# Two of a Strassen set's four differences in one VectorE step, on a decoder layer that keeps TensorE busy

## The chip, the cores and the metric

The kernel runs on one core of a Trainium2 chip. The metric is the device time of one execution in microseconds; the time before is the median of 3 runs. Engines are named as in the profile: PE is TensorE, PEld its weight loads, DVE is VectorE, ACT is ScalarE, POOL is GpSimd, and SP is SyncE, whose queue (SPq) issues most of the transfers. What can be told from no change on this kernel is about 0.2% (3.4 us).

## The reference

One decoder layer on 256 tokens of width 2048, all in float32, cut to what matters here:

```python
x = layer_norm(ALPHA * x + 0.5 * swiglu_ffn(x, ffn1...), ln1)      # FFN 1, inner width 5632
u = x @ w_in + b_in                                                # 2048 -> 3328
attn_out = sliding_window_attention_with_sinks(q, k, v, sinks)     # 16 heads of 64, window 128
conv_out = silu(layer_norm(depthwise_conv31(a * sigmoid(gate))))   # 1024 channels
x = layer_norm(ALPHA * x + concat(attn_out, conv_out) @ w_out + b_out, ln2)
x = layer_norm(ALPHA * x + 0.5 * swiglu_ffn(x, ffn2...), ln3)      # FFN 2
```

Here `swiglu_ffn(x) = (silu(x @ w_gate) * (x @ w_up)) @ w_down`. The weights (some 330 MB) are read once from memory, and every matrix product must be accurate to more than one pass of TensorE gives, so each operand is kept as a high part and a low part.

## The kernel before

**High and low parts.** Every weight unit of 128 x 1024 is loaded raw, cast by ACT to a high part (`hi`, line 171), and DVE makes its low part (`lo` = raw - hi, line 175). A product is then three matmuls (`mm3`, lines 678 to 680: hi x hi, lo of the weights, low of the activations), each 128 x 512. `hi` and `lo` are rings of 8 tiles.

**Strassen sets.** In both FFNs many units are not used as they are. Two raw units A = (a0 | a1) and B = (b0 | b1), halves of 512 columns, make a set (kind "S", 80 sets in all) whose seven products stand for eight; plain pairs of units are of kind "C". A set yields four units u0 to u3, made by the four jobs `zeroth`, `first`, `second` and `third` of the class `Steps`:

- u0 = (a0 | a1): a cast and a low part.
- u1 = (b0 - a0 | b1 - b0 + a0): the two differences t0 and t1 go into two tiles `sum` of 512 columns (tag "bc"), t1 from t0, then two casts and two low parts of 512.
- u2 = (b1 - b0 | b1): the difference is written over b0 in B's place (`more`), then one cast and one low part of 1024.
- u3 = (a1 - t1): written over a1, then a cast and a low part of 512.

In the trace, line 189 is a difference, 171 a cast and 175 a low part; `raw` is a unit of kind C, `more` one of a set's raw places, and `sum` a tile of t0 or t1. `more` has four places, room for two sets.

**What sets the order.** Nothing is scheduled by a compiler: each engine runs its instructions in the order in which the Python code issues them. While TensorE's products are issued, `pace` keeps a model of DVE's backlog (`vector` adds to it, `tensor` takes off) and issues the next job whenever the backlog is under 1.2 us. A low part is not issued with its cast but kept in `pending`, and goes out with a later job (`flush`) or when TensorE takes the unit (`take`). Between these DVE also has to empty the sums of the products (line 1078 in the up projection, line 939 in the down projection), to multiply the gates (`ht`, 1026), to transpose them in blocks (`hr`, 1040), and to split the result into `hh` and `hl` (1053 and 1054) when it is back from a round trip through memory (`far`, `hf`, issued by POOL).

**The mixer between the FFNs.** There the weights `in_win` are loaded by SP into four `raw` buffers, cast by ACT (line 254), and POOL makes the low parts (line 257). POOL also works the residual off, chunk by chunk (`residuals`, line 594: with a scale row `rg`, a shift row `rb` and a bias row `ro`, 512 columns each). These rows are loaded by SP too (`row_chunk`, line 476), into tiles of the same tag "bc" as the sums: six buffers of 512 columns before. ACT empties every projection (`part`, line 1259), does the exponentials of attention (line 1377) and scales its probabilities `pr` (line 1391) before TensorE transposes them (`tp`, line 1397).

Of the kernel before, what the change touches and what calls it, by code (L numbers as in the profile page):

```python
# [18 lines left out]
P = 128  # L19
# [35 lines left out]
BC = 6  # L55
# [29 lines left out]
class Steps:  # L85
# [66 lines left out]
    def load_set(self, n):  # L152

        k = 2 * (self.begun % 2)
        raws = [self.places[:, k], self.places[:, k + 1]]
# [3 lines left out]
        for raw, src in zip(raws, self.sources[n][0]):  # L159
            self.nc.sync.dma_start(raw, src)  # L160
# [3 lines left out]
    def upper(self, n, raw):  # L164

        pair = [self.pool.tile([P, 1024], F32R, tag=t, name=f"{t}{n}", bufs=RING) for t in ("hi", "lo")]
        raw = raw if isinstance(raw, list) else [raw]
        w = raw[0].shape[1]
        parts = [[x_, *(t[:, i * w : (i + 1) * w] for t in pair)] for i, x_ in enumerate(raw)]
        for x_, hi, lo in parts:  # L170
            self.nc.scalar.copy(hi, x_)  # L171

        def lower():
            for x_, hi, lo in parts:
                self.nc.vector.tensor_tensor(out=lo, in0=x_, in1=hi.bitcast(F32), op=ALU.subtract)  # L175
            self.vector(1.14 if len(raw) * w == 1024 else 0.6)
            self.ready[n] = pair
            while self.whole in self.ready:
                self.whole += 1
# [8 lines left out]
    def sub(self, out, a, b):  # L188
        self.nc.vector.tensor_tensor(out=out, in0=a, in1=b, op=ALU.subtract)  # L189
        self.vector(0.6)  # L190

    def zeroth(self, n, raws):
        zero = self.upper(n, raws[0])
        self.flush()
        raws.append(zero)

    def first(self, n, raws):
        a, b = ([r[:, :512], r[:, 512:]] for r in raws[:2])
        t = [self.act.tile([P, 512], F32, tag="bc", name=f"sum{n}", bufs=BC) for _ in range(2)]
        raws.append(t)  # L200
        self.sub(t[0], b[0], a[0])
        self.sub(t[1], b[1], t[0])
        self.pending = [raws[2], self.upper(n, t)]

    def second(self, n, raws):
        b = [raws[1][:, :512], raws[1][:, 512:]]
        self.sub(b[0], b[1], b[0])
# [3 lines left out]
    def third(self, n, raws):  # L211
        a1 = raws[0][:, 512:]
        self.sub(a1, a1, raws[3][1])
# [134 lines left out]
def hybrid_layer(  # L348
# [100 lines left out]
    def keep_tokens():  # L449
        for n in range(2 * NC_):  # L450
            b, cols = n // NC_, slice(n % NC_ * 512, (n % NC_ + 1) * 512)

            def one(b=b, cols=cols):
                t = act.tile([P, 512], F32, tag="bc", name="some", bufs=BC)
# [18 lines left out]

    def row_chunk(r, c, name, queue=nc.sync):
        t = act.tile([P, 512], F32, tag="bc", name=name, bufs=BC)
# [390 lines left out]
    def by_sums(kinds, blocks, out, shared):  # L866
# [17 lines left out]
        for n, kind in enumerate(kinds):  # L884
            if kind == "S":
# [4 lines left out]
                product(6, at("S2"), u[1], 1)  # L890
                u.append(st.take())
                product(7, at("S3"), u[2], 0)
# [304 lines left out]
def mixer(tc, nc, env):  # L1197
# [7 lines left out]
    with tc.tile_pool(name="mix", bufs=1) as pool:  # L1205
# [5 lines left out]
        bk = act.tile([P, 512], F32, tag="bc", name="bk", bufs=BC)  # L1211
# [386 lines left out]
```

## Time and profile before

| what | value |
|---|---|
| median of 3 runs | 1677.49 us (1676.08 to 1678.96) |
| the profiled execution | 1677.86 us, of which the span of instructions is 1676.10 us |
| PE busy | 1655.2 us, 99% of the span |
| DVE busy | 1485.0 us, 89% |
| ACT busy | 959.2 us, 57% |
| POOL busy | 322.6 us, 19%, nearly all of it in the mixer |
| granted TensorE clock | 0.998 |
| transfers | 377.31 MB, 225 GB/s |

A row of a group gives line, engine, operation, output and inputs, shapes and count, then the busy time and the mean of one in ns, then the idle time of the engine just before them and what ended it. A row of the timeline gives start, length, engine, line and operation, with the idle time before it in brackets; `x2` is two instructions merged into one row, the length from the first start to the last end. Ends of instructions on DVE overlap the next start a little, so what an instruction costs in a row of others is the step from start to start. A row of a window gives busy time and count of instructions for each engine.

### The profile page before, as it was taken

The page shows a single profiled execution, that of the slowest core. Times are in us where ns is not written, and L with a number is a line of the kernel's source. Part 1 is how long each engine was busy: PE and PEld are TensorE (multiplying, and loading weights), DVE is VectorE, ACT ScalarE, POOL GpSimd, SP SyncE. Part 2 cuts the span into 40 slices and gives each one's busy share as a digit, 9 for nine tenths or more (in the row PEclk, how much of TensorE's full clock was granted, in tenths as well). Part 3 has the DMA queues.
Part 4 walks back from the last instruction along what each step waited for, and adds up shares of the span by engine and source line. Part 5 has one row for each costly group of instructions (what it writes and reads, how often), then busy time and mean ns, then how long its engine had stood idle before and what let it go on. Part 6 is the DMA issues. An engine that isn't in the chain of part 4 may idle for free. (4 is left out here: it accounts for less than half of the span.)

```text
span 1676.1 us, 22034 instructions
## 1 busy us (share of the span) xinstructions
PE 1655.2 (99%) x7617; PEld 1369.7 (82%) x7617; DVE 1485.0 (89%) x2221; ACT 959.2 (57%) x1346; POOL 322.6 (19%) x302
## 2 busy tenths in 40 slices
PE   9999999999999999999999999999999999999996
PEld 7888888877778888888888888888888888788885
DVE  7899899999899998958888768899999999999987
ACT  6555555656555555676665466555555555555552
POOL 0100000111110001178996201000000000000012
PEclk9999999999999999999999999999999999999999
DMA  8666677677788567656655568666776666776675
GB/s 312 241 223 230 208 248 250 192 245 248 237 244 254 208 217 250 220 186 190 200 179 158 192 224 286 245 221 225 251 235 221 215 215 216 250 238 219 210 243 157
DMA packets 110976, 377.31 MB, mean 225 GB/s; under 512 B 13968, under 2 KB 14096, under 8 KB 110736
## 3 DMA queue, kind: packets, MB, share of 16 engines
q1 hardware_dynamic: 94032, 329.50, 56.9%
q0 software_dynamic: 16112, 45.10, 10.7%
q10 hardware_dynamic: 720, 1.31, 0.3%
q8 instruction: 59, 0.97, 0.2%
q14 instruction: 53, 0.43, 0.1%
HBM read 349.64 MB, written 27.26 MB: 225 GB/s over the span
## 5 line engine op out<-in xcount | busy, mean ns | idle before, releaser
L175 DVE TENSOR_TENSOR lo<-raw,hi 128x1024 fp32r<-128x1024 f32 x300 | 352.2, 1220 | 32.7 <-ACT hi L171 32.5
L678 PE MATMUL sum<-hi,xcat 128*128 128x512 f32 x956 | 372.0, 389 | 0.0
L679 PE MATMUL sum<-lo,xcat 128*128 128x512 f32 x956 | 371.9, 389 | 0.0
L680 PE MATMUL sum<-hi,xcat 128*128 128x512 f32 x956 | 371.9, 389 | 0.0
L171 ACT CAST hi<-more 128x1024 fp32r<-128x1024 f32 (+1 forms) x240 | 217.9, 908 | 251.6 <-DVE more L189 221.8
L171 ACT CAST hi<-raw 128x1024 fp32r<-128x1024 f32 x300 | 298.7, 1047 | 35.8 <-DMA raw<-in_wd 18.2
L175 DVE TENSOR_TENSOR lo<-more,hi 128x1024 fp32r<-128x1024 f32 (+1 forms) x240 | 244.3, 1041 | 20.3 <-ACT hi L171 20.2
L678 PE MATMUL sum<-hi,hh 128*128 128x512 f32 x580 | 226.5, 391 | 2.1 <-DVE part L939 2.1
L680 PE MATMUL sum<-hi,hl 128*128 128x512 f32 x580 | 226.0, 390 | 1.5 <-DVE hl L1054 1.5
L679 PE MATMUL sum<-lo,hh 128*128 128x512 f32 x580 | 226.0, 390 | 0.6 <-DVE lo L175 0.6
L254 ACT CAST hi<-raw 128x1024 fp32r<-128x1024 f32 (+1 forms) x156 | 158.6, 1029 | 93.1 <-PE acc L680 40.9
L678 PEld LDWEIGHTS sum<-hi,xcat 128*128 128x128 f32 x956 | 179.4, 188 | 37.6 <-issue 0.3
L680 PEld LDWEIGHTS sum<-hi,xcat 128*128 128x128 f32 x956 | 179.4, 188 | 37.5
L679 PEld LDWEIGHTS sum<-lo,xcat 128*128 128x128 f32 x956 | 179.4, 188 | 37.1
L257 POOL TENSOR_TENSOR lo<-raw,hi 128x1024 fp32r<-128x1024 f32 x73 | 176.0, 2438 | 110.8 <-ACT hi L254 103.8
L1045 POOL DMA_DIRECT2D far<-hr x88 | 49.1, 563 | 761.4 <-DVE hr L1040 761.3
L171 ACT CAST hi<-sum 128x512 fp32r<-128x512 f32 x160 | 98.9, 622 | 165.4 <-DVE sum L189 144.4
L678 PEld LDWEIGHTS sum<-hi,hh 128*128 128x128 f32 x580 | 108.8, 188 | 27.2 <-ACT hi L171 2.9
L680 PEld LDWEIGHTS sum<-hi,hl 128*128 128x128 f32 x580 | 108.9, 188 | 25.0 <-DVE hl L1054 2.4
L679 PEld LDWEIGHTS sum<-lo,hh 128*128 128x128 f32 x580 | 108.9, 188 | 24.1 <-DVE lo L175 1.7
L257 DVE TENSOR_TENSOR lo<-raw,hi 128x1024 fp32r<-128x1024 f32 (+1 forms) x83 | 98.1, 1201 | 23.9 <-ACT hi L254 23.6
L1078 DVE TENSOR_TENSOR part<-sum,part 128x512 f32<-128x512 f32 x152 | 101.4, 687 | 12.6 <-PE sum L680 7.8
(210 smaller groups left out, 2548.4 us busy)
## 6 DMA issues: line engine op xcount, KB each, us to landing
raw<-in_wu SPq DMA_DIRECT2D x244, 512.0 KB, 5.1
raw<-in_wd SPq DMA_DIRECT2D x120, 512.0 KB, 5.3
more<-in_wu SPq DMA_DIRECT2D x104, 512.0 KB, 6.8
more<-in_wd SPq DMA_DIRECT2D x56, 512.0 KB, 7.5
raw<-in_win SPq DMA_DIRECT2D x52, 512.0 KB, 4.2
raw<-in_wout SPq DMA_DIRECT2D x32, 512.0 KB, 3.8
far<-hr POOLq DMA_DIRECT2D x88, 128.0 KB, 2.7
hf<-far POOLq DMA_DIRECT2D x22, 512.0 KB, 4.9
```

The costliest lines, as they stand in the source:

```text
L171: self.nc.scalar.copy(hi, x_)
L175: self.nc.vector.tensor_tensor(out=lo, in0=x_, in1=hi.bitcast(F32), op=ALU.subtract)
L254: nc.scalar.copy(hi, raw)
L257: eng.tensor_tensor(out=lo, in0=raw, in1=hi.bitcast(F32), op=ALU.subtract)
L678: nc.tensor.matmul(ps, s_hi, m_hi, start=start, stop=False)
L679: nc.tensor.matmul(ps, s_hi, m_lo, start=False, stop=False)
L680: nc.tensor.matmul(ps, s_lo, m_hi, start=False, stop=stop)
L1045: nc.gpsimd.dma_start(far[:, :, t].rearrange("f r n -> r f n"), hr[32 * t : 32 * t + 32])
L1078: nc.vector.tensor_tensor(out=out, in0=ps, in1=other, op=ALU.add)
```

## The change

The set's units are cut in another way. One DVE instruction of 128 x 1024 makes d = (b0 - a0 | b1 - b0), reading B and a view of the two left halves (a0, b0) together. Then b0 is overwritten by (b1 - b0) + a0, so that u1 = d = (b0 - a0 | b1 - b0) and u2 = (b1 - b0 + a0 | b1). u1 so has one cast and one low part of 1024 in place of two of 512 each. The two products that use b1 - b0 and b1 - b0 + a0 change places (`product(7...)` and `product(6...)`). `zeroth` no longer flushes; `first` issues d, then flushes what is pending (the low part of the unit before), and then the step that depends on d. The tiles of tag "bc" become three of 1024 columns in place of six of 512: `row_chunk` hands out their halves in turn (`spare`), two row chunks to a tile; `some` and `bk` take a whole tile for one half.

```diff
--- before.py
+++ after.py
@@ -52,7 +52,7 @@
 PACE = 0.68
 STOCK = 3
 LAST = 8
-BC = 6
+BC = 3
 ORDER = "ccqqccqqccqqcc"
 CAP = 1.6
 FILL = 4.0
@@ -152,11 +152,11 @@
     def load_set(self, n):
 
         k = 2 * (self.begun % 2)
-        raws = [self.places[:, k], self.places[:, k + 1]]
+        raws = [self.places[:, k], self.places[:, k + 1], self.places[:, k : k + 2, :512]]
         self.begun += 1
         self.sets += 1
         self.loaded += 4
-        for raw, src in zip(raws, self.sources[n][0]):
+        for raw, src in zip(raws[:2], self.sources[n][0]):
             self.nc.sync.dma_start(raw, src)
         for i, work in enumerate((self.zeroth, self.first, self.second, self.third)):
             self.jobs.append((n + i, raws, work))
@@ -164,16 +164,12 @@
     def upper(self, n, raw):
 
         pair = [self.pool.tile([P, 1024], F32R, tag=t, name=f"{t}{n}", bufs=RING) for t in ("hi", "lo")]
-        raw = raw if isinstance(raw, list) else [raw]
-        w = raw[0].shape[1]
-        parts = [[x_, *(t[:, i * w : (i + 1) * w] for t in pair)] for i, x_ in enumerate(raw)]
-        for x_, hi, lo in parts:
-            self.nc.scalar.copy(hi, x_)
+        hi, lo = (t[:, : raw.shape[1]] for t in pair)
+        self.nc.scalar.copy(hi, raw)
 
         def lower():
-            for x_, hi, lo in parts:
-                self.nc.vector.tensor_tensor(out=lo, in0=x_, in1=hi.bitcast(F32), op=ALU.subtract)
-            self.vector(1.14 if len(raw) * w == 1024 else 0.6)
+            self.nc.vector.tensor_tensor(out=lo, in0=raw, in1=hi.bitcast(F32), op=ALU.subtract)
+            self.vector(1.14 if raw.shape[1] == 1024 else 0.6)
             self.ready[n] = pair
             while self.whole in self.ready:
                 self.whole += 1
@@ -185,32 +181,30 @@
             self.pending.pop(0)()
             most -= 1
 
-    def sub(self, out, a, b):
-        self.nc.vector.tensor_tensor(out=out, in0=a, in1=b, op=ALU.subtract)
+    def sub(self, out, a, b, op):
+        self.nc.vector.tensor_tensor(out=out, in0=a, in1=b, op=op)
         self.vector(0.6)
 
     def zeroth(self, n, raws):
-        zero = self.upper(n, raws[0])
+        raws.append(self.upper(n, raws[0]))
+
+    def first(self, n, raws):
+        d = self.act.tile([P, 2, 512], F32, tag="bc", name=f"sum{n}", bufs=BC)
+        b = raws[1].rearrange("p (h n) -> p h n", h=2)
+        self.nc.vector.tensor_tensor(out=d, in0=b, in1=raws[2], op=ALU.subtract)
+        self.vector(1.14)
         self.flush()
-        raws.append(zero)
-
-    def first(self, n, raws):
-        a, b = ([r[:, :512], r[:, 512:]] for r in raws[:2])
-        t = [self.act.tile([P, 512], F32, tag="bc", name=f"sum{n}", bufs=BC) for _ in range(2)]
-        raws.append(t)
-        self.sub(t[0], b[0], a[0])
-        self.sub(t[1], b[1], t[0])
-        self.pending = [raws[2], self.upper(n, t)]
+        self.sub(b[:, 0], d[:, 1], raws[0][:, :512], ALU.add)
+        raws.append(b[:, 0])
+        self.pending = [raws[3]] + [self.upper(n, d.rearrange("p h n -> p (h n)"))]
 
     def second(self, n, raws):
-        b = [raws[1][:, :512], raws[1][:, 512:]]
-        self.sub(b[0], b[1], b[0])
         self.pending.append(self.upper(n, raws[1]))
         self.flush(1)
 
     def third(self, n, raws):
         a1 = raws[0][:, 512:]
-        self.sub(a1, a1, raws[3][1])
+        self.sub(a1, a1, raws[4], ALU.subtract)
         three = self.upper(n, a1)
         self.flush(1)
 
@@ -451,7 +445,7 @@
             b, cols = n // NC_, slice(n % NC_ * 512, (n % NC_ + 1) * 512)
 
             def one(b=b, cols=cols):
-                t = act.tile([P, 512], F32, tag="bc", name="some", bufs=BC)
+                t = act.tile([P, 2, 512], F32, tag="bc", name="some", bufs=BC)[:, 0]
                 nc.gpsimd.dma_start(t, x[b * P : (b + 1) * P, cols])
 
                 def two():
@@ -471,8 +465,13 @@
                 cols = slice(h * 1024, (h + 1) * 1024)
                 nc.gpsimd.dma_start(xts[0][:, b, cols], side[b, :, cols])
 
+    spare = []
+
     def row_chunk(r, c, name, queue=nc.sync):
-        t = act.tile([P, 512], F32, tag="bc", name=name, bufs=BC)
+        if not spare:
+            both = act.tile([P, 2, 512], F32, tag="bc", name=name, bufs=BC)
+            spare.extend(both[:, h] for h in range(2))
+        t = spare.pop(0)
         queue.dma_start(t, rows[r, c * 512 : (c + 1) * 512].partition_broadcast(P))
         return t
 
@@ -887,9 +886,9 @@
                 u = [st.take() for _ in range(2)]
                 product(1, at("11"), u[0], 0)
                 product(5, at("S1"), u[1], 0)
-                product(6, at("S2"), u[1], 1)
+                product(7, at("S3"), u[1], 1)
                 u.append(st.take())
-                product(7, at("S3"), u[2], 0)
+                product(6, at("S2"), u[2], 0)
                 st.step(0)
                 product(2, at("12"), u[0], 1)
                 st.release()
@@ -1208,7 +1207,7 @@
         cv = pool.tile([P, NT, S], F32, name="cv")
 
 
-        bk = act.tile([P, 512], F32, tag="bc", name="bk", bufs=BC)
+        bk = act.tile([P, 2, 512], F32, tag="bc", name="bk", bufs=BC)[:, 0]
         nc.sync.dma_start(bk, env["b_tok"].partition_broadcast(P))
         grp = env["token_group"](x1, SKEW)
         kvq = pool.tile([P, 2, 512], F32, name="kvq")
```

The instructions of PE, POOL and SP stand in the same order as before. DVE has 164 rows fewer, ACT 82. Three places:

DVE in the up projection of FFN 1, at the set that stands at 347 us of the trace, before (`sum` is t0 or t1, `more` the set's places, `raw` the unit before the set):

```order
L175 TENSOR_TENSOR lo_3033<-raw_2919,hi_3032 128x1024
L189 TENSOR_TENSOR sum_3079<-more 128x512
L189 TENSOR_TENSOR sum_3080<-more,sum_3079 128x512
L175 TENSOR_TENSOR lo_3068<-more,hi_3067 128x1024
L1026 TENSOR_TENSOR ht<-part 128x8x32 x4
L1040 STREAM_TRANSPOSE hr<-ht 128x1024
L189 TENSOR_TENSOR more<-more 128x512
L175 TENSOR_TENSOR lo_3084<-sum_3079,hi_3083 128x512
L175 TENSOR_TENSOR lo_3084<-sum_3080,hi_3083 128x512
L189 TENSOR_TENSOR more<-more,sum_3080 128x512
L175 TENSOR_TENSOR lo_3127<-more,hi_3126 128x1024
```

and now (line 194 is d, 185 a difference, 171 a low part):

```order
L194 TENSOR_TENSOR sum_2994<-more 128x1024
L171 TENSOR_TENSOR lo_2957<-raw_2847,hi_2956 128x1024
L185 TENSOR_TENSOR more<-sum_2994,more 128x512
L1025 TENSOR_TENSOR ht<-part 128x8x32 x4
L1039 STREAM_TRANSPOSE hr<-ht 128x1024
L171 TENSOR_TENSOR lo_2992<-more,hi_2991 128x1024
L185 TENSOR_TENSOR more<-more 128x512
L171 TENSOR_TENSOR lo_3001<-sum_2994,hi_3000 128x1024
L171 TENSOR_TENSOR lo_3044<-more,hi_3043 128x1024
```

d has gone ahead of the low part of the unit before, the low part of u0 behind the gates and their transpose, the step on b0 ahead of them, and the step on a1 ahead of the low part of u1.

DVE in the down projection of FFN 1, around the last split into `hl` of a part (the set at 447 us of the trace), before:

```order
L175 TENSOR_TENSOR lo_3948<-more,hi_3947 128x1024
L175 TENSOR_TENSOR lo_3967<-sum_3962,hi_3966 128x512
L175 TENSOR_TENSOR lo_3967<-sum_3963,hi_3966 128x512
L1054 TENSOR_TENSOR hl_2325<-hf,hh_2324 128x512 x2
L189 TENSOR_TENSOR more<-more 128x512
L175 TENSOR_TENSOR lo_3997<-more,hi_3996 128x1024
L189 TENSOR_TENSOR more<-more,sum_3963 128x512
L175 TENSOR_TENSOR lo_4010<-more,hi_4009 128x512
```

and now:

```order
L185 TENSOR_TENSOR more<-sum_3858,more 128x512
L171 TENSOR_TENSOR lo_3844<-more,hi_3843 128x1024
L171 TENSOR_TENSOR lo_3862<-sum_3858,hi_3861 128x1024
L1053 TENSOR_TENSOR hl_2273<-hf,hh_2272 128x512 x2
L171 TENSOR_TENSOR lo_3889<-more,hi_3888 128x1024
L185 TENSOR_TENSOR more<-more 128x512
L171 TENSOR_TENSOR lo_3902<-more,hi_3901 128x512
```

The step that writes over b0 now stands two low parts ahead of the split, no longer between the split and the low part of u2 that waits for its cast.

SP in the mixer, at the third chunk of the residual (rows with what an instruction waits for), before:

```order
L476 DMA rg_2_7197<-in_rows 128x512
L476 DMA rb_2_7199<-in_rows 128x512
L476 DMA ro_2_7201<-in_rows 128x512
L115 DMA raw_7238<-in_win 128x1024 [waits DMAHW3_49,Pool_49]
```

and now (`rg_2` is the tile of the third chunk's scale and shift rows, `ro_2` the tile of its bias row):

```order
L475 DMA rg_2_7030<-in_rows 128x512 x2
L475 DMA ro_2_7033<-in_rows 128x512 [waits Pool_49]
L115 DMA raw_7070<-in_win 128x1024 [waits DMAHW3_49,Activation_49]
```

The order is the same, but the load of the third chunk's bias row now waits for POOL: its tile takes the place of the one that held the first chunk's bias row and the second chunk's scale row, and POOL reads the latter until the second chunk's last product with it.

## The prediction

> **What bounds the kernel now.** I read the shares of the engines first, then the windows, then the timeline of DVE and PE where a window falls short.
>
> ```profile
> span 1676.1 us, 22034 instructions
> PE 1655.2 (99%) x7617; PEld 1369.7 (82%) x7617; DVE 1485.0 (89%) x2221; ACT 959.2 (57%) x1346; POOL 322.6 (19%) x302
> ```
>
> PE is the bound, so the change can only win the time in which PE waits for an engine that it relieves, and can lose wherever it makes PE wait. Busy time hides short waits, since matmuls overlap; the count of matmuls in windows of 42 us does not:
>
> ```profile
> 84.00:126.00 42.00, 42.00 (x187) 34.77 (x186) 39.51 (x54) 23.79 (x32) 2.83 (x5) 1.00 0.66 223
> 336.00:378.00 42.00, 41.08 (x178) 32.83 (x177) 40.80 (x57) 25.60 (x35) 5.74 (x9) 1.00 0.76 244
> 378.00:420.00 42.00, 41.32 (x181) 33.49 (x180) 40.77 (x58) 25.04 (x35) 5.72 (x9) 1.00 0.78 245
> 420.00:462.00 42.00, 41.41 (x181) 33.25 (x179) 37.79 (x49) 23.62 (x32) 4.68 (x8) 1.00 0.73 239
> 462.00:504.00 42.00, 40.97 (x179) 33.06 (x178) 38.42 (x48) 22.87 (x28) 3.97 (x5) 1.00 0.81 243
> 630.00:672.00 42.00, 41.22 (x182) 33.79 (x181) 35.90 (x47) 22.52 (x30) 4.92 (x9) 1.00 0.72 253
> 1344.00:1386.00 42.00, 41.38 (x182) 33.90 (x182) 40.76 (x58) 24.05 (x32) 2.78 (x5) 1.00 0.64 225
> 1428.00:1470.00 42.00, 40.97 (x179) 33.02 (x179) 39.40 (x50) 23.87 (x29) 3.54 (x4) 1.00 0.71 231
> 1596.00:1638.00 42.00, 41.24 (x182) 33.82 (x181) 35.54 (x45) 23.22 (x29) 5.47 (x10) 1.00 0.73 241
> ```
>
> An undisturbed FFN window holds 187 matmuls, 42/187 = 0.225 us each. The eight others fall 9, 6, 6, 8, 5, 5, 8 and 5 short: 52 x 0.225 = 11.7 us. That is all that a faster DVE can win; the clock column is 1.00 in each. The last window (from 1638) has no sets in it and is left alone.
>
> **The change part by part.** First DVE's own price. One set at 347 us:
>
> ```profile
> 345.99 1.22 DVE L175 TENSOR_TENSOR lo<-raw,hi 128x1024 fp32r<-128x1024 f32 x1
> 347.13 0.69 DVE L189 TENSOR_TENSOR sum<-more 128x512 f32<-128x512 f32 x1
> 347.85 0.69 DVE L189 TENSOR_TENSOR sum<-more,sum 128x512 f32<-128x512 f32 x1
> 348.46 1.22 DVE L175 TENSOR_TENSOR lo<-more,hi 128x1024 fp32r<-128x1024 f32 x1
> 349.59 1.42 DVE L1026 TENSOR_TENSOR ht<-part 128x256 f32<-128x256 f32 x4
> 351.05 1.25 DVE L1040 STREAM_TRANSPOSE hr<-ht 128x1024 f32<-128x1024 f32 x1
> 352.22 0.65 DVE L189 TENSOR_TENSOR more<-more 128x512 f32<-128x512 f32 x1
> 352.79 1.28 DVE L175 TENSOR_TENSOR lo<-sum,hi 128x512 fp32r<-128x512 f32 x2
> 353.99 0.69 DVE L189 TENSOR_TENSOR more<-more,sum 128x512 f32<-128x512 f32 x1
> 354.59 1.22 DVE L175 TENSOR_TENSOR lo<-more,hi 128x1024 fp32r<-128x1024 f32 x1
> ```
>
> From start to start a 1024 takes 1.14 us (345.99 to 347.13), a 512 takes 0.60 (353.99 to 354.59), and 0.72 where the next one depends on it (347.13 to 347.85). The five instructions that change cost 0.72 + 4 x 0.60 = 3.12. Now d, the step on b0 and one low part cost 1.14 + 0.60 + 1.14 = 2.88, or 3.00 where no low part is waiting and the step stands right behind d. So 0.12 to 0.24 us per set, 10 to 19 us over 80 sets; nearly all of it beside PE's work, since PE loses 11.7 us in all. ACT's casts go from two to one; ACT is 57% busy, and I cost that at nothing.
>
> On this the Trainium skill (VectorE: DVE Perf Modes, "The DRAIN you can't avoid") says that a semaphore between VectorE instructions costs nothing extra, since the pipe drains either way. The trace differs: 0.72 against 0.60. By the rule a set would save 0.12 us everywhere, and the sum below would be some 0.3 us smaller.
>
> The work does not only shrink, it moves. At this place d now stands ahead of the C unit's low part, and the low part of u0 behind the gates (2.63 us, 349.59 to 352.22). From 345.99: d 1.14, C 1.14, b0 0.60, gates and transpose 2.63, u0 1.14, a1 0.60, low part of u1 1.22 to its end: 354.46, where its first half ended at about 353.5 before. PE needs that one first and the low part of u2 six matmuls (1.35 us) later: 355.81. Before, u2's ended at 354.59 + 1.22 = 355.81. So here the saving is given back by the order, and PE gains only what the sets ahead saved, about 0.2 us. I take 0.2 to 0.25 for each of the four waits in the windows at 336 (two), 378 and 1344: **0.8 us** of 4.5. Bounds: 0, if DVE was not late from the sets ahead but from the split into `hl`; 4.5, if all goes.
>
> The other kind of place:
>
> ```profile
> 452.10 1.30 DVE L1054 TENSOR_TENSOR hl<-hf,hh 128x512 fp32r<-128x512 f32 x2 [1.32 <-ACT hh L1053]
> 453.31 0.68 DVE L189 TENSOR_TENSOR more<-more 128x512 f32<-128x512 f32 x1
> 455.24 1.23 DVE L175 TENSOR_TENSOR lo<-more,hi 128x1024 fp32r<-128x1024 f32 x1 [1.25 <-ACT hi L171]
> 457.81 0.69 DVE L175 TENSOR_TENSOR lo<-more,hi 128x512 fp32r<-128x512 f32 x1 [0.74 <-ACT hi L171]
> 456.52 0.50 PE L679 MATMUL sum<-lo,hh 128*128 128x512 f32 x1 [0.36 <-DVE lo L175]
> 459.00:475.20 16.20, 15.61 (x68) 12.14 (x66) 15.94 (x20) 10.71 (x14) 1.75 (x2) 1.00 0.71 213
> 475.47 0.47 PE L678 MATMUL sum<-hi,hh 128*128 128x512 f32 x1 [0.86 <-DVE part L939]
> ```
>
> Here b0 is written behind the split, its cast follows, and DVE idles 1.25 us for it, and 0.74 for the next one's; PE waits for both. Now b0 is written two low parts earlier and only the cast stands behind the cast of `hh`, so u2's low part can start at about 453.7, 1.5 us earlier, and u3's 1.5 to 1.9. PE's 1.35 us in window 420 go. DVE is then busy 15.94 of 16.20 us up to 475.2, where PE waits for it to empty a sum; it arrives 1.9 us earlier there, of which PE has used 1.35, and one set more saves 0.1 to 0.2. Windows 420 and 462 together: **2.0 us** of 3.2. In FFN 2 the first of these waits is not there but the second is (window 1428, 8 short): all of it, **1.7**. Windows 630 and 1596 (PE waits for `hl` behind a row of low parts; two sets ahead) take 0.4 each: **0.8**. Sum of the gains 0.8 + 2.0 + 1.7 + 0.8 = **5.3 us**; bounds 1.9 (2.0 and 1.7 halved, the rest nothing) and 11.7.
>
> Then the buffers. With three "bc" tiles, the bias row of the third chunk in the mixer waits for POOL's last product with the second chunk's scale row:
>
> ```profile
> 801.66 0.43 SPq L476 DMA_DIRECT2D ro<-in_rows  x1
> 803.24 0.33 SPq L115 DMA_DIRECT2D raw<-in_win  x1
> 809.13 1.31 POOL L594 TENSOR_TENSOR xt<-xt,rg 128x512 f32<-128x512 f32 x1
> raw<-in_win SPq DMA_DIRECT2D x52, 512.0 KB, 4.2
> 808.62 1.05 ACT L254 CAST hi<-raw 128x1024 fp32r<-128x1024 f32 x1 [0.92 <-DMA raw<-in_win]
> 809.58 0.62 ACT L600 ACTIVATE rb<-rb 128x512 f32<-128x512 f32 x1
> 813.69 0.37 ACT L1259 COPY part<-in_c 128x256 f32<-128x256 f32 x1 [3.49 <-PE in_c L1247]
> 816.50:827.40 10.90, 10.90 (x64) 9.59 (x63) 6.76 (x27) 10.44 (x32) 10.05 (x6) 1.00 0.51 159
> 825.85 1.49 ACT L1391 ACTIVATE pr<-pr,sm 128x128 f32<-128x128 f32 x4
> 827.45 1.25 PE L1397 MATMUL tp<-ident,pr 128*128 128x128 f32 x10
> ```
>
> SP would stand from 801.66 to 809.13 + 1.31 = 810.44, 8.8 us, and behind it stand the loads of the weights. The first goes out at about 811.2 in place of 803.24. Landing took 4.2 us in the median, and 5.3 for this one (its cast began at 808.62 when it landed): 815.4 to 816.5. ACT's cast then holds the queue: behind it the scaling of a row (0.62), the emptying of `in_c` (0.37), and, through DVE, the exponentials. Cast 1.05 + 0.62 + 0.37 puts the emptying's end at 817.4 to 818.5, where it was 814.06: 3.4 to 4.4 late. From 816.5 to 827.4 ACT is busy 10.44 of 10.90 us, so it makes up some 0.4, and the scaling of the second head's `pr`, which ended at 827.34, ends 3 to 4 us later. PE's transposes of it come at about 828.2, 0.8 after: PE loses 2.2 to 3.2. I take **2.5**; bounds 0 (if a slack on ACT or PE that these rows don't show takes it) and 8.8, the wait itself, if nothing behind it is made up. The low parts of this stage have their ring of 8 ahead, and I cost their delay at nothing; if that cover were gone, the same 8.8 bounds it. The Trainium skill (DMA: Bandwidth & Descriptors, "Anatomy of one DMA — SWDGE (gpsimd) path") states that a semaphore wait happens on the issuing sequencer and never in the DMA engines; no run here shows a wait of this length on SP yet.
>
> `some` in FFN 1 takes a whole tile too, and eight d's now wait for its transfer out. The closest pair:
>
> ```profile
> 330.01 0.88 POOL L459 DMA_DIRECT2D y<-some  x1 [13.65 <-ACT some L458]
> y<-some POOLq DMA_DIRECT2D x8, 256.0 KB, 8.3
> ```
>
> It lands at about 330.0 + 8.3 = 338.3; the d that waits would start at 346. So nothing. d also waits for both raw places, as t0 did.
>
> **The sum.** 1677.86 (the profiled execution: span 1676.10 and 1.76 around it) - 5.3 + 2.5 = 1675.1. The median stands 0.4 below that execution: **1674.8 us**, 0.16% faster, inside the 0.2% (3.35 us) that a measurement can tell.
>
> **The rivals.**
>
> *The SP wait is hidden.* Then only the gains are left: 1677.5 - 5.3 = 1672.2. For it: a ring of 8 low parts stands between POOL and PE. Against: PE's transposes (827.45) stand 0.1 us behind ACT's `pr` (827.34), and no ring lies between these two.
>
> *DVE's lateness is a chain that shortens everywhere.* All 11.7 us go, 1677.5 - 11.7 + 2.5 = 1668.3. For it: windows 336, 378 and 1344 have DVE 97% busy (40.8 of 42). Against: the order above.
>
> *DVE's lateness starts at the round trip through memory,* so that saved steps become idle time ahead of the next split: gains 1, loss 2.5: 1679. For it: the 1.32 us wait for `hh`.
>
> *Slower: the SP wait goes through whole.* POOL, ACT and PE each fall behind by the wait, 8.8 us, and the gains are the small ones: 1677.5 - 1.9 + 8.8 = 1684.4. It decides once the loss is over the gains by 3.35 us, so from about 5.3 us of PE time at 801 to 830 with those gains. For it: POOL is busy 10.05 of 10.90 us there. Against: it has slack to PE of some units.
>
> *The change does nothing:* the low parts wait for casts or transfers as before; 1677.5. The wait rows at 455 and 457 speak against it.
>
> **How the numbers follow.** Forecast 0.46 (of it 0.05 beyond 1674.1, so faster), SP wait hidden 0.24, everything shortens 0.09, round trip 0.09, slower 0.09, nothing 0.03. Faster by over 0.2%: 0.05 + 0.24 + 0.09 = 0.38; slower 0.09; within 0.2%: 0.53. The range reaches from between the two faster rivals to the round trip's case: 1670.5 to 1679.5.
>
> **What would show it.** The group of `sum` differences on DVE is 80 of 128x1024 at about 1.22 us; the low part of u2 no longer waits 1.25 us for its cast; windows at 420, 462 and 1428 come back to 186 or 187 matmuls, those at 336, 378 and 1344 only by one or two. SP's `ro` at about 800 takes some 9 us, and PE idles 2 to 3 us at its transposes near 825. No PE gap there makes me wrong by 2.5 us; windows 336 and 378 at 187 make me wrong by up to 4.

## The result, and the profile after

| | median | runs | ratio to before, 95% interval |
|---|---|---|---|
| before | 1677.63 us | 7 (1676.08 to 1679.12) | |
| the change | **1672.02 us** | 7 (1667.91 to 1675.23) | **0.9964 (0.9952 to 0.9975)** |
| the change, measured again beside other kernels | 1670.63 us | 5 (1668.91 to 1674.42) | 0.9961 (0.9948 to 0.9974) |

The change makes the kernel 0.25 to 0.48% faster, some 6 us. 1674.8 was forecast; the time lies in the range (1670.5 to 1679.5), but 2.8 us under the forecast, and it is a gain that a measurement can tell, where "no change that can be told" was given the larger chance.

The profiled execution took 1669.45 us. The windows of its trace (time, then busy time and instructions of PE, PEld, DVE, ACT and POOL, then clock, DMA share and GB/s):

```profile
336.00:378.00 42.00, 42.00 (x187) 34.75 (x187) 40.59 (x51) 25.08 (x32) 5.73 (x9) 1.00 0.77 254
378.00:420.00 42.00, 42.00 (x187) 34.79 (x186) 40.91 (x52) 25.08 (x32) 5.72 (x9) 1.00 0.80 250
798.00:840.00 42.00, 39.25 (x249) 33.84 (x249) 30.38 (x93) 25.97 (x55) 36.67 (x20) 1.00 0.59 176
1344.00:1386.00 42.00, 42.00 (x187) 34.78 (x186) 40.90 (x52) 24.00 (x31) 2.78 (x5) 1.00 0.63 225
```

All eight FFN windows that fell short hold 187 matmuls, also 420, 462, 630, 1428 and 1596, which are not shown; and in the mixer PE stands for 2.75 us, where before it did not stand at all:

```profile
798.00:840.00 42.00, 42.00 (x266) 36.58 (x265) 34.89 (x104) 27.09 (x59) 41.16 (x23) 1.00 0.68 202
```

That is the rival "a chain that shortens everywhere", and one could stop here. But a second profile of the same kernel has these windows:

```profile
336.00:378.00 42.00, 41.10 (x180) 33.16 (x179) 40.63 (x52) 24.73 (x32) 5.73 (x9) 1.00 0.77 246
378.00:420.00 42.00, 41.45 (x183) 33.99 (x182) 40.90 (x52) 25.23 (x33) 5.73 (x9) 1.00 0.78 251
462.00:504.00 42.00, 41.84 (x184) 34.14 (x183) 39.38 (x44) 23.13 (x26) 3.52 (x4) 1.00 0.85 261
630.00:672.00 42.00, 42.00 (x187) 34.75 (x187) 35.99 (x43) 22.11 (x27) 4.92 (x9) 1.00 0.70 236
1344.00:1386.00 42.00, 42.00 (x187) 34.79 (x186) 40.91 (x52) 23.98 (x31) 2.78 (x5) 1.00 0.65 225
```

Here 336 and 378 come back by two matmuls each only (178 and 181 before). The first profile was a lucky one; what went with it is shown below.

A count that does not depend on where a window begins: the trace of every kernel here has 7617 matmuls in the same order, but for the two products of a set that change places with each other, so the time from the start of one to the start of another compares a stage between kernels. FFN 1 is here from matmul 1300 to 3050 (297 to 701 us before; matmul 1300 starts at 296 to 298 us in every trace, so next to nothing is won or lost ahead of it), the mixer's part with the late load from 3500 to 4100 (778 to 871 us), FFN 2 from 4700 to 7500 (999 to 1638 us). Worked out from the traces, us:

| profile | FFN 1 | mixer | FFN 2 | time of this execution |
|---|---|---|---|---|
| before | 404.2 | 93.06 | 638.7 | 1677.86 |
| before, second profile | 404.0 | 93.05 | 639.2 | 1678.33 |
| the change | 396.4 | 96.45 | 634.7 | 1669.45 |
| the change, second profile | 399.8 | 96.34 | 634.7 | 1670.63 |

In the stages that take 396.4 and 634.7 us the trace shows no wait of PE. So the FFNs win 4.2 to 7.7 and 4.0 to 4.5 us, and the mixer loses 3.3 to 3.4.

On DVE the groups (line, operation, tiles, shapes, count, busy time, mean ns, idle time before them) of the change are, in the second profile:

```profile
L171 DVE TENSOR_TENSOR lo<-more,hi 128x1024 fp32r<-128x1024 f32 x160 | 195.0, 1219 | 2.6 <-ACT hi L168 2.6
L171 DVE TENSOR_TENSOR lo<-raw,hi 128x1024 fp32r<-128x1024 f32 x300 | 354.0, 1219 | 39.5 <-ACT hi L168 39.5
L194 DVE TENSOR_TENSOR sum<-more 128x1024 f32<-128x1024 f32 x80 | 97.1, 1214 | 2.8 <-DMA more<-in_wd 1.8 <-DMA more<-in_wu 1.0
```

and of the kernel before:

```profile
L175 DVE TENSOR_TENSOR lo<-more,hi 128x1024 fp32r<-128x1024 f32 x160 | 195.1, 1219 | 12.6 <-ACT hi L171 12.5
L175 DVE TENSOR_TENSOR lo<-raw,hi 128x1024 fp32r<-128x1024 f32 x300 | 352.2, 1220 | 32.7 <-ACT hi L171 32.5
```

80 steps d at 1.21 us, as foreseen. DVE's idle time ahead of the low parts of 1024 of the sets' places fell from 12.6 to 2.6 us: these were the waits of 1.25 us for the cast of u2. That of u3, ahead of the low parts of 512, stayed (7.7 to 7.4, not shown). The idle time ahead of the low parts of kind C (`raw`) rose meanwhile from 32.7 to 39.5 us: a DVE that is less late stands idle elsewhere, so the sum of its idle time for casts hardly fell, and only where PE waits behind such a wait is its end a gain. In all DVE has 160 instructions fewer than before (2221 to 2061) and ACT 80 (1346 to 1266), two and one for each set; the 164 and 82 of the section on the change don't stand in the trace.

In the mixer of the first profile after (the SP queue, then POOL, ACT, DVE and PE):

```profile
792.60 1.68 SPq L475 DMA_DIRECT2D rg<-in_rows  x2
803.05 0.33 SPq L475 DMA_DIRECT2D ro<-in_rows  x1
803.48 19.62 SPq L115 DMA_DIRECT2D raw<-in_win  x8
801.76 1.26 POOL L593 TENSOR_TENSOR xt<-xt,ro 128x512 f32<-128x512 f32 x1
809.34 1.05 ACT L248 CAST hi<-raw 128x1024 fp32r<-128x1024 f32 x1 [9.03 <-DMA raw<-in_win]
818.94 0.38 ACT L1258 COPY part<-in_a 128x256 f32<-128x256 f32 x1
819.35 0.49 DVE L1263 SCALAR_TENSOR_TENSOR in_a<-in_a,bias,part 128x256 f32<-128x256 f32 x1 [3.36 <-ACT part L1258]
820.44 2.09 PE L1248 MATMUL in_a<-xcat,hi 128*128 128x512 f32 x8 [2.38 <-DVE sm L1383]
```

SP stands from 794.3 to 803.05, 8.8 us, and goes on when POOL has ended the product that was named, at 803.02 (the profile calls its tile `ro`, after the bias row that took the tile first; the half that is read here is the scale row). The load behind it goes out, ACT idles 9.03 us for it, empties `in_a` late, DVE with it, and PE waits 2.38 us until DVE is through. (The profile names a later step, `sm`. That PE waits until `in_a` is read is inferred: its next product writes `in_a`, and the last DVE step that reads it, L1328, runs from 819.87 to 820.29.) What the prediction says there of the Trainium skill (DMA: Bandwidth & Descriptors, "Anatomy of one DMA — SWDGE (gpsimd) path"), that a wait is the issuing sequencer's, can now be seen: the load itself took 5.8 us (issued at 803.48, its cast 809.34), 0.5 more than was counted; the rest of the delay is that it had not been issued.

### The profile page after: what moved, and what is told of

It reads as the page before. It is cut to its first block, busy times and chain, and to the rows that moved or that the text cites. A ratio compares the mean times of both kernels' runs of the same rounds, so it can differ in the third digit from the quotient of the medians.

```text
span 1667.7 us, 21771 instructions
## 1 busy us (share of the span) xinstructions
PE 1650.7 (99%) x7617; PEld 1371.7 (82%) x7617; DVE 1470.8 (88%) x2061; ACT 941.6 (56%) x1266; POOL 323.0 (19%) x302
## 5 line engine op out<-in xcount | busy, mean ns | idle before, releaser
L168 ACT CAST hi<-sum 128x1024 fp32r<-128x1024 f32 x80 | 84.3, 1053 | 173.2 <-DVE sum L194 166.5
```

Source lines behind the costliest of these rows:

```text
L168: self.nc.scalar.copy(hi, raw)
```

## Experiments

Four questions: does the wait on SP cost the 3.3 us; which part of the change wins in the FFNs; why do the two profiles of one kernel differ; and is it DVE's work at all.

### The rows in the mixer

**By kind.** The changed kernel, with the halves of a tile given to rows that are released together:

```diff
-    spare = []
+    spare = {}
 
     def row_chunk(r, c, name, queue=nc.sync):
-        if not spare:
+        left = spare.setdefault(name[:2] == "ro", [])
+        if not left:
             both = act.tile([P, 2, 512], F32, tag="bc", name=name, bufs=BC)
-            spare.extend(both[:, h] for h in range(2))
-        t = spare.pop(0)
+            left.extend(both[:, h] for h in range(2))
+        t = left.pop(0)
```

> The changed kernel with one edit: the halves of a tile for row chunks are handed out by kind, so that scale and shift row of a chunk share a tile and the bias rows of two chunks share another. The load of the third chunk's bias row then waits for the two additions of bias rows, which POOL has behind it 16 us earlier (786.2 of the trace after), and no longer for the product with the second chunk's scale row. If the wait on SP costs PE what stands in the profile after (2.4 + 0.4 us at the first products of the mixer's projections), this kernel is 2.5 to 2.8 us faster than the changed one, about 1669.3 us, and the window at 798 has 12 matmuls more. If PE loses that time there for another reason (the order of POOL's work, the next load), the time stays at 1672. If the wait went through whole it would be 8.8 us faster, 1663.

Measured: 1664.78 us (1664.61 to 1667.11), 0.9926 of before (0.9911 to 0.9941). SP no longer stops:

```profile
794.15 2.10 SPq L476 DMA_DIRECT2D rg<-in_rows  x2
796.29 0.43 SPq L476 DMA_DIRECT2D ro<-in_rows  x1
797.38 22.75 SPq L115 DMA_DIRECT2D raw<-in_win  x8
```

The mixer's stage takes 93.05 us again, so the wait on SP is what cost 3.3 to 3.4 us there. The median fell by more than that, 7 us, so the same kernel was measured again:

> The kernel with the rows handed out by kind again, unaltered. Against the change as measured twice (1672.0 and 1670.6) it should win the 3.3 us of the mixer stage: 1667.3 to 1668.7. If its first median (1664.8) comes again, it wins 6 to 7 us, and about 3 of them are not the wait in the mixer.

Measured: 1667.35 us (1665.51 to 1668.46), 0.9945 (0.9932 to 0.9957), mixer 93.05. Against the change (0.9964, 0.9961) the two measurements together give 0.27% with an uncertainty of about half of it, 4.5 us +- 2; 3.3 lies in it. The first median was low, as it seems by chance. This kernel beats both others: 9 to 12 us faster than before.

**The buffers alone.** The kernel before, with the changed kernel's tiles and t0 and t1 in the halves of one:

```diff
-BC = 6
+BC = 3
-        t = [self.act.tile([P, 512], F32, tag="bc", name=f"sum{n}", bufs=BC) for _ in range(2)]
+        both = self.act.tile([P, 2, 512], F32, tag="bc", name=f"sum{n}", bufs=BC)
+        t = [both[:, h] for h in range(2)]
```

(with `row_chunk`, `some` and `bk` as in the change)

> The kernel before with the changed kernel's buffers alone: three tiles of 1024 columns, row chunks in their halves in turn, t0 and t1 of a set in two halves of one tile; every instruction of the sets as before. If the buffers cost what SP's wait costs PE in the mixer, it is 2.5 to 2.8 us slower than before, about 1680.3 us, with the FFN windows as before. If the wait is hidden, 1677.6; whole, 1686.

Measured: 1681.89 us (1676.45 to 1683.69), 1.0023 (1.0013 to 1.0033), 3.9 us +- 1.7 slower. The mixer's stage takes 96.37 us, 3.3 more; FFN 1 404.4 and FFN 2 638.8 as before. No other cost or gain of the buffers shows.

### Order or merging

The change does two things to the sets: it merges instructions, and it moves steps (b0 early, a waiting low part between d and the step that needs it). Each alone:

**Merged, in the old places.**

```diff
     def zeroth(self, n, raws):
-        raws.append(self.upper(n, raws[0]))
+        zero = self.upper(n, raws[0])
+        self.flush()
+        raws.append(zero)
 
     def first(self, n, raws):
...
-        self.flush()
-        self.sub(b[:, 0], d[:, 1], raws[0][:, :512], ALU.add)
-        raws.append(b[:, 0])
+        raws.append(d)
...
     def second(self, n, raws):
+        b0 = raws[1][:, :512]
+        self.sub(b0, raws[4][:, 1], raws[0][:, :512], ALU.add)
+        raws.append(b0)
```

> The changed kernel with the old places of the steps: the first job flushes the low part of the unit before, the second makes d and nothing else, and the step on b0 comes in the third, right ahead of the cast of u2, as before. Merged instructions as in the change: 1.14 + 0.60 + 1.14 = 2.88 us a set in place of 3.12. If the work saved on DVE is what counts (0.24 us a set, summed up over the sets since DVE last stood idle), it keeps nearly all of the gain: 1672 to 1673 us. If the place of the step on b0 is what counts, as in the prediction for the windows at 420 and 1428 (2.0 + 1.7 us), it is 3 to 4 us slower than the change, 1675 to 1676, and the waits of 1.25 and 0.74 us for the casts of u2 and u3 are back.

Measured: 1681.27 us (1677.92 to 1684.32), 1.0024 (1.0014 to 1.0034).

**The order, in pieces of 512.**

```diff
-        self.nc.vector.tensor_tensor(out=d, in0=b, in1=raws[2], op=ALU.subtract)
-        self.vector(1.14)
+        for h in range(2):
+            self.sub(d[:, h], b[:, h], raws[2][:, h], ALU.subtract)
         self.flush()
```

(and two casts and two low parts for u1, as before)

> The changed kernel with d, its cast and its low part in two instructions of 512 each; the order of the change stays, the step on b0 early and a low part ahead of it where one waits. Per set 5 x 0.60 = 3.00 us in place of 2.88 (before: 3.12, since t1 stood right behind t0 and needed it). If the order alone is what counts, it is as fast as the change, 1672 to 1673 us. If DVE's work counts, half of the saving is given back: some 4 of the 8.4 us that the FFNs won, 1676.

Measured: 1675.05 us (1670.85 to 1678.05), 0.9987 (0.9976 to 0.9997). DVE is hardly relieved in this order: in 53 of the 80 sets the step on b0 stands right behind the second half of d, which it needs, and takes the place of the dependent pair of before (0.72 us from start to start, in both), so the 3.00 us of the expectation hold in 27 sets only, and 27 x 0.12 = 3 us of DVE's work are saved. Both kernels carry the mixer's loss, so both were run with the rows by kind too:

> As merge_only (merged instructions, old places of the steps), with the rows handed out as in pairs. By 3.3 us for the wait 1678, no faster than before (1677): the merging alone is worth nothing, and the order decides. By 7 us 1674, and the merging alone is worth 3 us.

Measured: 1677.6 us (1674.54 to 1681.12), 1.0003 (0.9994 to 1.0012).

> As order_only (the change's order, d with its cast and low part in pieces of 512), with the rows handed out as in pairs, so that the mixer's wait is out of the comparison. If that wait costs 3.3 us in each kernel: 1675.0 - 3.3 = 1671.8 us, so the merging of instructions is worth 7 us on top of the order (1664.8). If the wait costs what pairs won on the change (7 us): 1668, and the merging is worth 3 us.

Measured: 1670.09 us (1668.09 to 1672.23), 0.9954 (0.9940 to 0.9967). With the mixer's loss out of it, as a share of the time before:

| | pieces of 512 | merged |
|---|---|---|
| old places | 1 (before) | 1.0003 |
| new places | 0.9954 | 0.9926 and 0.9945 |

The order wins 0.46%, 7.7 us; with the mixer's loss in both kernels it is 0.36% (0.9987 against the 1.0023 of the buffers alone). Since it saves only 3 us of DVE's work, it wins by its places. Which of the moved steps wins is not separated. The merging wins nothing in the old places that these medians can tell, and 0.1 to 0.3% more in the new ones: 0.9926 is clear of 0.9954, 0.9945 is not, and with the mixer's loss in both it is 0.23 to 0.26% (0.9964 and 0.9961 against 0.9987). That the merged kernel in the old places would keep "nearly all of the gain" was wrong; that the places count was right, and they count for twice the 3 to 4 us that were expected.

Why does merging win nothing by itself? In its trace (old places, merged, rows by kind) DVE and ACT at the set at 332 us:

```profile
332.22 1.22 DVE L196 TENSOR_TENSOR sum<-more 128x1024 f32<-128x1024 f32 x1
333.36 1.22 DVE L171 TENSOR_TENSOR lo<-more,hi 128x1024 fp32r<-128x1024 f32 x1
335.10 2.87 DVE L1081 TENSOR_TENSOR part<-sum,part 128x512 f32<-128x512 f32 x4 [0.52 <-ACT part L1087]
333.53 1.05 ACT L168 CAST hi<-sum 128x1024 fp32r<-128x1024 f32 x1 [2.66 <-DVE sum L196]
334.49 0.57 ACT L1087 COPY part<-sum 128x512 f32<-128x512 f32 x1
```

The cast of u1 stands on ACT ahead of the copy that DVE's sums need, and it cannot begin before the whole of d is there. Before, the cast of t0 began while DVE made t1:

```profile
333.60 0.69 DVE L189 TENSOR_TENSOR sum<-more,sum 128x512 f32<-128x512 f32 x1
333.66 1.29 ACT L171 CAST hi<-sum 128x512 fp32r<-128x512 f32 x2 [2.19 <-PE sum L680]
```

So d makes ACT late, and DVE waits 0.52 us. The change has the same cast and the same copy, but DVE has the step on b0 to do meanwhile (first profile):

```profile
330.40 1.22 DVE L194 TENSOR_TENSOR sum<-more 128x1024 f32<-128x1024 f32 x1
331.65 0.69 DVE L185 TENSOR_TENSOR more<-sum,more 128x512 f32<-128x512 f32 x1
332.26 1.22 DVE L171 TENSOR_TENSOR lo<-more,hi 128x1024 fp32r<-128x1024 f32 x1
333.40 2.86 DVE L1077 TENSOR_TENSOR part<-sum,part 128x512 f32<-128x512 f32 x4
331.71 1.05 ACT L168 CAST hi<-sum 128x1024 fp32r<-128x1024 f32 x1 [2.08 <-DVE sum L194]
332.66 0.58 ACT L1083 COPY part<-sum 128x512 f32<-128x512 f32 x1
```

Over the whole trace DVE's waits for that copy (line, releaser, us, times, longest) are, merged in the old places:

```profile
DVE part L1081 <- ACT part L1087: 7.9, 17, 0.5
DVE part L942 <- ACT part L948: 4.2, 8, 0.5
```

and in the change, second profile:

```profile
DVE part L1077 <- ACT part L1083: 0.6, 3, 0.2
```

Before the change it was

```profile
DVE part L1078 <- ACT part L1084: 1.1, 5, 0.2
```

Merging takes 0.24 us of work from DVE in the 55 sets where another step follows d, and 0.12 in the 25 where the step on b0 does: 16 us. Of these 11 come back as waits for ACT, and the 12.5 us of idle time ahead of the low part of u2 stay as well. What is left is small: FFN 2 takes 637.5 us in both kernels that are merged in the old places, 1.2 to 1.7 less than before; FFN 1 takes 403.4 and 409.0, the latter in an execution in which three more read-backs landed late (6.6 to 8.0 us; more on these below), so there it can't be told. The prediction put ACT's casts at nothing, "ACT is 57% busy"; busy shares do not show that ACT stood on a path from DVE to DVE.

**d alone merged.** There was another explanation, from the prediction itself: u1's low part in one piece comes late for PE. So the old places with d merged, and cast and low part of u1 in two:

```diff
-        self.pending = [raws[3]] + [self.upper(n, d.rearrange("p h n -> p (h n)"))]
+        self.pending = [raws[3]] + [self.upper(n, [d[:, h] for h in range(2)])]
```

> The old places of the steps and the rows by kind, as in pairs_merge_only, with d in one instruction, but its cast and its low part in two of 512 as before, so that the half of u1 that PE needs first is ready 0.6 us sooner. DVE: 1.14 + 3 x 0.60 = 2.94 us a set (before 3.12, pairs_merge_only 2.88). If merging won nothing in the old order (1677.6 against 1677.0 before) because u1's whole low part gives the saving back, as the prediction argued for the windows at 336, 378 and 1344, this kernel keeps the saving: 0.18 us a set are 14 us of DVE, and DVE's work counted 0.4 to 1 in PE's in the runs with more of it (0.12 us a set 3 us, 0.35 us a set 12 us): about 1672 us. If the late step on b0 and DVE's idle time for its cast (12.7 us) swallow the saving, it stays at 1677.

Measured: 1679.32 us (1676.87 to 1681.64), 1.0013 (1.0005 to 1.0022). As the whole reason that explanation falls: with the first half ready sooner nothing is won. The waits for the copy are even longer (ACT now has two casts ahead of it):

```profile
DVE part L1085 <- ACT part L1091: 9.2, 17, 0.6
DVE part L946 <- ACT part L952: 5.0, 8, 0.6
```

### Is it DVE's work?

The order could have won by its places alone. So, in the kernel with the rows by kind, more work for DVE at the same places:

```diff
         self.vector(1.14)
+        self.nc.vector.tensor_tensor(out=d[:, 0, :256], in0=b[:, 0, :256], in1=raws[2][:, 0, :256], op=ALU.subtract)
         self.flush()
```

> The kernel with the rows handed out by kind, and one more DVE step of 128 x 256 in each set, right behind d, that writes a quarter of d once more with the same values: about 0.35 us a set from start to start, so 3.23 us a set in place of 2.88 (before: 3.12; d in pieces: 3.00), in the order of the change. If DVE's work is what makes PE wait, it is slower than the one with d in pieces (1670.1), by its 0.12 us to 5 us about 1675 or more, and windows 336, 378 and 462 fall short again. If the order of the steps decides alone, it stays at 1665 to 1668.

Measured: 1678.99 us (1676.77 to 1681.78), 1.0016 (1.0007 to 1.0026); FFN 1 takes 407.6 us and FFN 2 641.5. The step costs more than the 0.35 us of the expectation, since it also waits for d: from d to the next old step it is 1.71 us in place of 1.25 (53 sets) and 1.59 in place of 1.13 (27), so 0.46 us a set. 80 x 0.46 = 37 us of DVE cost 12 to 14 us. Windows 336, 378 and 462 hold 184, 177 and 178 matmuls, and windows that were full fall short:

```profile
420.00:462.00 42.00, 39.54 (x171) 31.47 (x171) 36.37 (x45) 21.57 (x29) 4.29 (x7) 1.00 0.68 229
630.00:672.00 42.00, 40.48 (x179) 33.06 (x178) 36.21 (x44) 19.70 (x25) 4.94 (x9) 1.00 0.70 246
1344.00:1386.00 42.00, 40.68 (x179) 32.95 (x178) 40.84 (x53) 23.15 (x30) 2.79 (x5) 1.00 0.61 211
```

DVE waits no longer for ACT's copy here than in the change (0.6 us in all), so it is not the later cast that costs. So DVE's time does count, about a third of it; the places decide whether a saving reaches PE.

### Two profiles of one kernel

The expectations here count the read-back's landing "after the transpose"; their 8.4 and 10.8 to 12.5 us are counted from the end of the issue of the last of the four writes to memory. From the transpose's end it is 2.7 us more. "Fourth" counts from nought: it is the fifth of the eleven read-backs of FFN 1.

> The changed kernel again, unaltered. In its first profile the read-back of the fourth part of FFN 1 landed 8.4 us after the transpose, in the other five kernels profiled so far 10.8 to 12.5; DVE stood idle 2 to 3.2 us for it in those, and PE then lost 1.8 us or more up to the down projection. If the late landing is the usual case, this second profile shows it (DVE idle some 2 us at about 321, windows 336 and 378 at 181 to 183 matmuls) and a time of about 1671 us; if the first profile was the usual case, 187 in all windows again. With pairs at 1664.8 and 3.3 us of PE's time in the mixer the median should be 1668; if it stays at 1672, the wait on SP costs more in most executions than in the profiled one, or another loss comes with it.

Measured: 1670.63 us; the windows are shown above. DVE at the fourth part's split, in this profile:

```profile
317.96 1.22 DVE L171 TENSOR_TENSOR lo<-more,hi 128x1024 fp32r<-128x1024 f32 x1
322.11 0.49 DVE L1001 TENSOR_TENSOR sums<-hf 128x128 f32<-128x128 f32 x2 [2.93 <-DMA hf<-far]
```

In the first profile after there was no such wait (319.47, right behind the low part). So the late landing is the usual case, and in it PE still waits at the set at 347 us, for u1's low part (made from 353.15 to 354.37):

```profile
354.42 0.50 PE L678 MATMUL sum<-lo,xs 128*128 128x512 f32 x1 [0.90 <-DVE lo L171]
```

> The kernel before again, for a second profile. If its short windows are not chance, they stand where they stood: 336, 378, 420, 462, 630, 1344, 1428 and 1596, some 50 matmuls in all, and the fourth read-back lands over 10.8 us after the transpose.

Measured: the windows at 336, 378, 462, 630, 1344, 1428 and 1596 fall short by 9, 6, 8, 5, 4, 8 and 5 matmuls, as in the first profile, 420 by 4 (6), and one at 84, full in the first, by 5. The read-back lands late, DVE idles 2.59 us.

> The kernel with the rows handed out by kind, with part of the computation left out: the first four of the eight pieces in which POOL's queue fetches the input tokens and adds them to their copy in memory are not moved, so that no such transfer follows the read-backs of the fourth part. If those transfers (256 KB each, issued 0.65 and 1.3 us behind the read-back) hold it up, it lands about 8 us after the transpose in place of 10.8 to 12.5, DVE does not stand idle 2 to 3 us at 321, and PE's stage over the windows at 336 to 420 comes to 158.7 us in place of 160.4 to 161.4: 1.8 to 2.7 us faster than with all pieces. If the weight loads of SP hold it up, it lands as late as before.

Measured: 1665.35 us (1664.24 to 1668.26), 0.9932 (0.9917 to 0.9947), no wait at 321, windows 336 and 378 without a wait. FFN 1 still took 399.7 us, since another read-back, issued at 442, landed late in this execution (8.3 us; DVE idles 4.2). At 321 this looks like a yes, but it is not one, and the time is that of the kernel with all pieces (1664.8 and 1667.4). Set side by side, the 14 profiles divide by something else: when the read-back goes out against SP's burst of weight loads. One that landed late, before, and one early, the change (POOL, then SP):

```profile
314.17 0.57 POOL L1047 DMA_DIRECT2D hf<-far  x1 [3.72 <-DMA far<-hr]
313.14 3.73 SPq L115 DMA_DIRECT2D raw<-in_wu  x4
```

```profile
313.40 0.57 POOL L1046 DMA_DIRECT2D hf<-far  x1 [3.33 <-DMA far<-hr]
313.30 4.87 SPq L115 DMA_DIRECT2D raw<-in_wu  x4
```

In 11 profiles the burst's first load (512 KB) had gone out 0.6 to 1.25 us ahead of the read-back, and the read-back took 7.0 to 8.7 us to land. In three (the change's first, the one with more work on DVE, and this one) the first load went out 0.1 us ahead of it or later, and the read-back took 4.8 to 5.8 us. The token pieces were moved in two of these three. Other read-backs of the same traces point the same way. Three that stand where no token piece is near (at 568 and 572 us in the two kernels merged in the old places, at 1313 in the one with the order in pieces and the rows by kind) went out 0.6 to 0.7 us behind the first load of a burst and took 6.6 to 7.8 us, where in the other profiles the same read-backs went out at most 0.33 us behind one and took 4.4 to 5.5. So the weight loads are the better explanation. It is not a rule without exception (one read-back took 8.0 us only 0.42 us behind a load), what makes the writes before the read-back land up to 1.7 us sooner in some executions is not shown, and no run here moves one of the two alone.

## Why the prediction was right and where it was wrong

- **Windows 420 and 1428, 2.0 + 1.7 us with 462.** Right in mechanism and nearly in size: the step on b0 no longer stands between the split and its low part, the 10 us of idle time for casts are gone, 420 and 1428 are full. 462 wins 1.1 us in the second profile (179 to 184) where 0.65 were counted. The kernel with the order alone has this gain, those in the old places have not.
- **Windows 336 and 378, 0.6 us of the 0.8.** In the usual case right: 178 to 180 and 181 to 183, 4 x 0.225 = 0.9 us. PE then waits for u1's low part, which the prediction named as the late one. What it had only as a bound and as the round-trip rival, at 0.09, is that the rest hangs on the landing of one read-back, 2.3 us of DVE's idle time at 321.88 in the trace before; the row was there to be read.
- **Windows 1344, 630 and 1596: the step that failed.** "PE gains only what the sets ahead saved, about 0.2 us", and 0.4 each for 630 and 1596: 1.0 us together. Measured: all three full, 0.9 to 1.1 us each. The order at the place itself was read rightly. From the sums to the low part of u2 it was, before:

```profile
1346.54 1.88 DVE L1078 TENSOR_TENSOR part<-sum,part 128x512 f32<-128x512 f32 x3
1356.94 1.82 DVE L175 TENSOR_TENSOR lo<-more,hi 128x1024 fp32r<-128x1024 f32 x2
```

10.40 us, and in the change's second profile 10.26:

```profile
1343.87 1.88 DVE L1077 TENSOR_TENSOR part<-sum,part 128x512 f32<-128x512 f32 x3
1354.13 1.82 DVE L171 TENSOR_TENSOR lo<-more,hi 128x1024 fp32r<-128x1024 f32 x2
```

But DVE arrives there earlier by more than one set's saving. Counted by PE's matmuls in the two second profiles, the sum ahead of those three came 6 matmuls earlier, 1.35 us, and so it did in the groups ahead of the waits of 630 and 1596. Followed back in these two traces, and counted against PE, the change's DVE is level with before at the sums that begin at 1293.69, 1.4 us ahead at the gates at 1306.50, 1.0 at the split, 0.7 at the sums at 1335.89, 1.4 at 1342.14 and 1.6 at the low part of u2 at 1354.13, where PE lost 0.9 before. So the saving of some four sets adds up, and DVE carries it across idle time at the split:

```profile
1321.96 0.69 DVE L1053 TENSOR_TENSOR hl<-hf,hh 128x512 fp32r<-128x512 f32 x1 [0.63 <-ACT hh L1052]
```

DVE waits there for ACT's `hh`, which runs from 1321.31, right behind a cast (from 1320.35) that waited for DVE's step on b0; the read-back had landed at 1320.33, so it was not what held it. One or two sets' saving was the wrong term.
- **DVE's price per set, 0.12 to 0.24 us.** Right in the trace: d to the step that depends on it takes 1.25 us (330.40 to 331.65), d to another step 1.13. The step on b0 stands right behind d in 53 of the 80 sets, so the larger saving comes in 27 only: 27 x 0.24 + 53 x 0.12 = 13 us in all. By the sentence of the Trainium skill (VectorE: DVE Perf Modes, "The DRAIN you can't avoid") that a semaphore costs nothing extra, the two would be equal; here too the trace differs.
- **ACT at nothing.** Right for the change, wrong as a reason: the merged cast does stand on DVE's path, and only the order covers it (waits of 12.1 us in the old places, 0.6 in the change).
- **The mixer, 2.5 us.** The mechanism was right to the wait's length (8.8 us) and its end, and "hidden" and "whole" both fell. The size was 3.3 to 3.4, just over the upper end of the 2.2 to 3.2 that was worked out. PE's wait was not at the transposes of `pr` near 825 but at `in_a` at 820.44, by the emptying of a sum: the same late ACT, met at the first place where PE needs it.
- **The sum.** Gains 5.3 forecast, 38 matmuls or 8.6 us in the second profile; loss 2.5 forecast, 3.3 measured; net 2.8 against 5.3. Both terms were too small, the gain by 3.3 and the loss by 0.8, so the errors cancel in part, and that is luck. (The terms as written give 1674.7, not 1674.8.)
- **The rivals.** "Everything shortens" is what the first profile shows and not what the second does, and its own loss was too small. "Round trip" came true at one place: at the read-back at 322 DVE idles 2.93 us where it idled 2.29 and 2.59 before, and 336 and 378 win two and two matmuls. At the split at 1322 the saving is handed on. "Does nothing" and "slower" fell.

## What to carry to other kernels

An engine that is 97% busy is late by a sum over many steps: cost a saving there over all steps since it last waited for something that its own steps do not set, not over the one ahead of the wait, and look at the order of its steps before work to merge: here the order won 0.46% and merging alone nothing. Merging two instructions makes whoever reads the first half wait for the whole; put independent work behind it, or the saving turns into a wait. Two halves of a shared tile should go to data that are released together, above all where the waiting load holds a queue.

## What the runs showed of the hardware that was not expected

The read-back of a part (128 x 1024, float32) took 4.8 to 5.8 us when it went out no more than 0.1 us behind the first of a burst of weight loads, and 7.0 to 8.7 us when it went out 0.6 to 1.25 us behind it, in all 14 profiles (the fourth part of FFN 1). A microsecond of order between two queues went with 2 to 3 us of DVE's time, and in the change with 2.7 us of PE's between the second profile and the first in the stage that follows (161.4 against 158.7 us from matmul 1300 to 2000). That this explains the spread between executions of one kernel (7 us in the change's seven) is likely, but was only argued.
